# A two-group decoder step on one core: a per-tile head and two more FFN steps in a woven attention stretch

## The chip, the core and the metric

The kernel runs on one core of a Trainium2 chip. The metric is the device time of one execution in microseconds. The median of three runs of the kernel before is 2487.3 us (2486.04 to 2487.68). A core has a matmul engine (PE, with PEld for its weight loads), a vector engine (DVE), a scalar engine (ACT), a general engine (POOL) and a queue engine that issues transfers (SP). Each works through its own instructions in order; where one needs another's result it waits.

## What is computed

One inference step of a decoder trunk with two layers over two groups: a prompt of 1024 tokens and 8 samples of one token, with width 1024, all in float32. Layer 0 mixes by a gated recurrence, layer 1 by stick-breaking attention over keys and values that all tokens share; both add attention into 256 memory tokens and a SwiGLU FFN, with a norm before and after each sub-layer. Cut to what matters here:

```python
def rmsnorm(x, g):
    y = xf * lax.rsqrt(jnp.mean(xf * xf, axis=-1, keepdims=True) + EPS)
    return (y * g).astype(x.dtype)

def swiglu(h, w_gu, w_down):
    gate, up = jnp.split(h @ w_gu, 2, axis=-1)
    return (jax.nn.silu(gate) * up) @ w_down

for l in range(DEPTH):
    hn = rmsnorm(h, g[0])
    if l < N_A:
        mix, S = a_mixer(hn, w_in_a[l], ...)
    else:
        mix = b_mixer(hn, w_in_b[l - N_A], sb_bias[l - N_A], k_all, v_all, ...)
    h = h + rmsnorm(mix, g[1])
    h = h + rmsnorm(swiglu(rmsnorm(h, g[2]), w_gu[l], w_down[l]), g[3])
```

## The kernel before

The prompt is cut into two groups of 512 tokens; the 8 samples ride with group 1, whose tiles are 520 wide. Activations lie with the 1024 features in eight blocks `x0` to `x7` of 128 rows. Each float32 operand is split into a rounded high part (ACT, `L204`, `L225`, `L1024`) and the rest (DVE, `L205`, `L226`, `L1025`), and each product is three matmuls: high by high, high by low, low by high. A weight tile of 256 KB is loaded by SP, split by ACT and DVE, and used by PE.

**The head** (`start(0, ...)`, `L317` on). Four tiles of 128 tokens are loaded. `rms_rows` squares a tile and sums it (on ACT at `L310`, for every second tile on DVE at `L308`), takes the root by a logarithm and an exponential on ACT (`L311`, `L312`) and scales the tile on DVE (`L313`). Then, for each of the eight feature blocks, four transposes on PE (`L340`) fill one bank, and ACT and DVE scale and split it into `x` (`L343`, `L344`). The norm gains come from `par`, a transpose of the packed parameters (`L148`, `L149`). The first products are those for V (`rows_proj`, `L1017`): eight weight tiles, twelve matmuls each at `L1030`.

**Weaving.** A stage is a generator that yields after each step. `weave` always takes the next step of the stream whose number of steps taken over its weight is smallest; a stream that runs out drops away. This fixes the order in which work is handed over. The framework then places the instructions on each engine, which moves some of them past each other, and the engines keep that order.

**Layer 1, group 1 attention** (`L1570`). Three streams are woven: prompt attention (`sb_prompt`, 28 steps, and `mem_attn`, 8) with weight 40; sample attention (38 steps) with weight 39; and the FFN of group 0 with weight 30. A step of `sb_prompt` makes scores on PE (`L1324`), a bias and clip on DVE (`L1335` to `L1339`), an exponential and a logarithm on ACT (`L1310`, `L1311`), a scan and a subtraction on DVE (`L1344`, `L1346`), an exponential on ACT (`L1347`), four transposes on PE (`L1353`), a copy on ACT (`L1355`) and the value matmuls on PE (`L1358`). Sample steps put products and sums on DVE (`L924`, `L925`, `L936`, `L937`) and a small matmul on PE (`L938`).

The FFN (`class ffn`, `L688`) is cut into five parts of 5, 5, 4, 4 and 4 hidden blocks. A part makes one step for each hidden block (gate and up, 48 matmuls of 512 columns) and four steps for the down-projection (two output blocks each, 24 matmuls, added to the residual by DVE at `L391`). Parts 0 to 2 and the first 4 steps of part 3, its hidden blocks, run in this weave: 9 + 9 + 8 + 4 = 30 steps. The other 4 steps of part 3 are held back.

**After it.** `o1.mm` is the output projection of group 1. `o1.finish` (17 steps) takes its norm (the sum over partitions is a matmul at `L247`, root at `L248`, `L249`), adds the residual in eight steps (`L372`, `L378`, squares summed at `L258`), takes the next norm and scales and splits the eight blocks (`normed`: `L264`, `L225`, `L226`) that the last FFN reads. It is woven, 17 to 12, with the 4 steps of part 3 that were held back and the 8 of part 4. Then the last FFN begins (`ffn_w`, `L1578`): three hidden blocks by plain products (`gate_up_q`, `L455`; their up halves are multiplied in at `L468`), during which DVE also prepares sums of the normed blocks (`sums_w`, `L289`, `L297`), and from the fourth block on products by these sums (`gate_up_w`, `L502`). `f0.finish` and the stores of group 0 are woven into it.

```python
    weave(
        (chain(b1.sb(), b1.mem()), 40), (chain(b1.sb_sample(), b1.mem_sample()), 39),
        (chain(f0.part(0), f0.part(1), f0.part(2), islice(p3, 4)), 30),
    )
    o1 = out_proj(1, 1, A, True)
    weave((o1.mm(b1.xo), 8), (ws, 9))
    weave((o1.finish(), 17), (chain(p3, f0.part(4, True)), 12))
```

Of the kernel before, what the change touches and what calls it, by code (L numbers as in the profile page):

```python
# [23 lines left out]
def tile_decoder(  # L24
# [25 lines left out]
    def nm(s):  # L50
        uid[0] += 1
        return f"{s}_{uid[0]}"
# [45 lines left out]
    def NS():  # L98
        return nsp.tile([P, 512], F32, tag="ns", name=nm("ns"))
# [21 lines left out]
    def S():  # L121
        return smp.tile([P, 512], F32, tag="s", name=nm("s"))
# [21 lines left out]
    nc.vector.memset(epsb, EPS)  # L144
    xsraw = const.tile([P, ND, NB], F32, name="xsraw")
    par = const.tile([P, P], F32, name="par")
    pp = S()
    nc.tensor.transpose(pp[:, :P], prow, ident)  # L148
    nc.scalar.copy(par, pp[:, :P])  # L149

    def gcol(l, i, k):
        o = (l * 4 + i) * ND + k
# [151 lines left out]
    def rms_rows(xt, n, dve=False):  # L304
        ss = small([P, 1], tag="rr")
        junk = M().rearrange("p a n -> p (a n)")[:n, :D]
        if dve:
            nc.vector.tensor_tensor_reduce(junk, xt, xt, 1.0, 0.0, ALU.mult, ALU.add, ss[:n])  # L308
        else:
            nc.scalar.activation(junk, xt, AF.Square, accum_out=ss[:n])  # L310
        nc.scalar.activation(ss[:n], ss[:n], AF.Ln, scale=1.0 / D, bias=epsb[:n])  # L311
        nc.scalar.activation(ss[:n], ss[:n], AF.Exp, scale=-0.5)  # L312
        nc.vector.tensor_scalar(xt, xt, ss[:n], None, op0=ALU.mult)  # L313

    made, now = [None], [None]

    def start(g, out):  # L317
        if g:
            xtok.append(rpool.tile([P, CH, D], F32, tag="r", name="xtok1"))
            for tb in range(CH):  # L320
                nc.sync.dma_start(xtok[g][:, tb, :], x_prompt[0, g * G + tb * P : g * G + (tb + 1) * P, :])
            xs = C().rearrange("p a n -> p (a n)")[:NB]
            nc.sync.dma_start(xs, x_sample.rearrange("b o d -> (b o) d"))
        for tb in range(CH):
            rms_rows(xtok[g][:, tb, :], P, g == 0 and tb % 2 == 1)
            yield
        if g:
            ps = S()
            for k in range(ND):
                nc.tensor.transpose(ps[:, k * NB : (k + 1) * NB], xs[:, k * P : (k + 1) * P], ident[:NB, :NB])  # L330
            nc.vector.tensor_copy(xsraw, ps[:, : ND * NB].rearrange("p (k t) -> p k t", k=ND))
            rms_rows(xs, NB)
            pn = S()
            for k in range(ND):
                nc.tensor.transpose(pn[:, k * NB : (k + 1) * NB], xs[:, k * P : (k + 1) * P], ident[:NB, :NB])
            yield
        for k in range(ND):
            ps = S() if k % 2 else NS()
            for tb in range(CH):
                nc.tensor.transpose(ps[:, tb * P : (tb + 1) * P], xtok[g][:, tb, k * P : (k + 1) * P], ident)  # L340
            x = X(g)
            gk = gcol(0, 0, k)
            nc.scalar.activation(x[:, 0, :G], ps, AF.Copy, scale=gk)  # L343
            made[0] = nc.vector.scalar_tensor_tensor(  # L344
                x[:, 1, :G], ps, gk, x[:, 0, :G].bitcast(F32), op0=ALU.mult, op1=ALU.subtract
            )
            if g:
                pk = pn[:, k * NB : (k + 1) * NB]
                nc.scalar.activation(x[:, 0, G:], pk, AF.Copy, scale=gk)
                nc.vector.scalar_tensor_tensor(  # L350
                    x[:, 1, G:], pk, gk, x[:, 0, G:].bitcast(F32), op0=ALU.mult, op1=ALU.subtract
                )
            out.append(x)
            yield
# [662 lines left out]
    def rows_proj(W, m0, xt, dst):  # L1017

        pb = [mmp.tile([P, 2, 512], F32, tag="mm", name=nm("mm")) for _ in range(2)]
        for k in range(ND):  # L1020
            raw = wraw.tile([P, 512], F32, tag="w", name=nm("w"))
            nc.sync.dma_start(raw, W[k * P : (k + 1) * P, m0 : m0 + H * P])
            ws = wspl.tile([P, 2, 512], F32R, tag="ws", name=nm("ws"))
            nc.scalar.copy(ws[:, 0, :], raw)  # L1024
            nc.vector.tensor_sub(ws[:, 1, :], raw, ws[:, 0, :].bitcast(F32))  # L1025
            for i in range(2):
                for wi, (xi, s) in enumerate(((0, 0), (1, 0), (0, 1))):
                    for a in range(2):
                        c = 2 * i + a
                        nc.tensor.matmul(  # L1030
                            pb[i][:, a, :], xt[k][:, xi, c * P : (c + 1) * P], ws[:, s, :],
                            start=(k == 0 and wi == 0), stop=(k == ND - 1 and wi == 2),
                        )
            if k % 2:
                yield
        nc.scalar.copy(dst[0][:, :, :512], pb[0])
        nc.vector.tensor_copy(dst[1][:, :, :512], pb[1])
# [493 lines left out]
    def rest():  # L1531
# [36 lines left out]
    f0 = ffn(0, 1, o0.x)  # L1568
    p3 = f0.part(3)
    weave(  # L1570
        (chain(b1.sb(), b1.mem()), 40), (chain(b1.sb_sample(), b1.mem_sample()), 39),
        (chain(f0.part(0), f0.part(1), f0.part(2), islice(p3, 4)), 30),
    )
    o1 = out_proj(1, 1, A, True)
    weave((o1.mm(b1.xo), 8), (ws, 9))
# [37 lines left out]
```

## Time and profile before

| | us |
|---|---|
| median of three runs | 2487.3 |
| the profiled execution | 2488.67 |
| its span, first to last instruction | 2487.0 |
| V phase of the head ends | 39.39 |
| attention of layer 1, group 1, woven with the FFN | about 1597 to 1950 |
| `o1.mm` and `o1.finish` with the rest of the FFN | 1950 to 2110.05 |
| the last FFN begins | 2110.05 |

The profile is one execution. The page shows the busy time of each engine; the chain that ended last, followed back from the end; groups of instructions with their line. Views by stretch give, for a window, the busy time of PE, PEld, DVE, ACT and POOL with the number of instructions in brackets, then the granted PE clock (1.00 is full), the share of the transfer engines and their GB/s. Views in order of time give start, duration, engine, line, operation, written tile `<-` read tiles, sizes, and in brackets the idle time just before and who ended it. Matmuls overlap, so their single durations are longer than their pace; the pace is a stretch over its count.

### The profile page before, as it was taken

The page shows a single profiled execution, that of the slowest core. Times are in us where ns is not written, and L with a number is a line of the kernel's source. Part 1 is how long each engine was busy: PE and PEld are TensorE (multiplying, and loading weights), DVE is VectorE, ACT ScalarE, POOL GpSimd, SP SyncE. Part 2 cuts the span into 40 slices and gives each one's busy share as a digit, 9 for nine tenths or more (in the row PEclk, how much of TensorE's full clock was granted, in tenths as well). Part 3 has the DMA queues.
Part 4 walks back from the last instruction along what each step waited for, and adds up shares of the span by engine and source line. Part 5 has one row for each costly group of instructions (what it writes and reads, how often), then busy time and mean ns, then how long its engine had stood idle before and what let it go on. Part 6 is the DMA issues. An engine that isn't in the chain of part 4 may idle for free.

```text
span 2487.0 us, 42201 instructions
## 1 busy us (share of the span) xinstructions
PE 2456.4 (99%) x15971; PEld 2177.2 (88%) x15971; DVE 1615.4 (65%) x2942; ACT 1213.0 (49%) x2328; POOL 178.8 (7%) x316
## 2 busy tenths in 40 slices
PE   8999999999999999999999999999999999999998
PEld 6888888877879998899999989876777888999998
DVE  5867556754777685655755675777687466855666
ACT  5437544243435554555444554554554445654445
POOL 1000101100000000111200102111000100000000
PEclk9999999999999999999999999999999999999999
DMA  5354666546745437767666649745253473464552
GB/s 188 114 166 111 158 190 157 133 129 163 213 146 144 141 119 224 202 163 184 163 194 172 195 127 276 226 143 154 80 175 113 131 203 119 142 187 146 147 148 74
DMA packets 530503, 395.29 MB, mean 159 GB/s; under 512 B 21237, under 2 KB 468802, under 8 KB 530298
## 3 DMA queue, kind: packets, MB, share of 16 engines
q1 hardware_dynamic: 501114, 312.88, 42.2%
q0 software_dynamic: 29184, 79.70, 13.9%
q8 instruction: 126, 2.06, 0.3%
q14 instruction: 79, 0.65, 0.1%
HBM read 362.69 MB, written 101.11 MB: 186 GB/s over the span
## 4 chain that ended last, share of the span: by engine, by line
PE 89%; DVE 5%; DMA 2%; issue 2%; ACT 2%; POOL 0%; SPq 0%; DVEq 0%; POOLq 0%; ACTq 0%
PE mm L218 48%; PE q L502 13%; PE q L639 8%; PE s L1162 2%; PE mm L1030 2%; PE q L455 2%; PE s L897 1%; PE s L866 1%; PE s L1358 1%; PE mm L815 1%; PE mm L842 1%; PE s L1324 1%; PE q L671 1%; PE s L890 1%; PE ns L938 1%
## 5 line engine op out<-in xcount | busy, mean ns | idle before, releaser
L218 PE MATMUL mm<-x,ws 128*128 128x260 f32 (+1 forms) x6240 | 1120.7, 336 | 1.7 <-DVE r L648 1.7
L218 PEld LDWEIGHTS mm<-x,ws 128*128 128x128 f32 x6240 | 940.8, 188 | 134.6 <-issue 10.3
L204 ACT CAST ws<-w 128x512 fp32r<-128x512 f32 (+1 forms) x652 | 382.9, 588 | 549.6 <-PE mm L218 382.9
L205 DVE TENSOR_TENSOR ws<-w,ws 128x512 fp32r<-128x512 f32 (+1 forms) x652 | 419.8, 648 | 276.6 <-ACT ws L204 265.8
L218 PE MATMUL mm<-m,ws 128*128 128x512 f32 (+1 forms) x1344 | 281.1, 361 | 0.1
L218 PEld LDWEIGHTS mm<-m,ws 128*128 128x128 f32 x1344 | 217.8, 188 | 39.5 <-issue 4.5
L639 PE MATMUL q<-m,ws 128*128 128x260 f32 (+1 forms) x1824 | 222.1, 282 | 0.3 <-DVE r L648 0.3
L639 PEld LDWEIGHTS q<-m,ws 128*128 128x128 f32 x1824 | 219.0, 188 | 1.8 <-DVE t L525 0.5
L493 DVE TENSOR_TENSOR ws<-w,ws 128x512 fp32r<-128x512 f32 x181 | 124.1, 690 | 90.2 <-ACT ws L492 86.5
L492 ACT CAST ws<-w 128x512 fp32r<-128x512 f32 x181 | 111.9, 621 | 105.9 <-PE q L639 34.5
L502 PE MATMUL q<-x,ws 128*128 128x260 f32 (+1 forms) x1188 | 157.8, 282 | 0.0
L502 PEld LDWEIGHTS q<-x,ws 128*128 128x128 f32 x1188 | 148.6, 188 | 0.0
L502 PE MATMUL q<-y,ws 128*128 128x260 f32 x912 | 119.4, 283 | 0.5 <-DVE t L468 0.5
L502 PEld LDWEIGHTS q<-y,ws 128*128 128x128 f32 x912 | 113.5, 188 | 0.8 <-DVE t L468 0.8
L455 PE MATMUL q<-x,ws 128*128 128x260 f32 (+1 forms) x720 | 88.9, 283 | 0.0
L455 PEld LDWEIGHTS q<-x,ws 128*128 128x128 f32 x720 | 87.0, 188 | 1.1 <-issue 0.9
L502 PE MATMUL q<-a,ws 128*128 128x260 f32 (+1 forms) x672 | 87.1, 282 | 0.7 <-DVE t L468 0.7
L502 PEld LDWEIGHTS q<-a,ws 128*128 128x128 f32 x672 | 83.2, 188 | 0.9 <-DVE t L468 0.9
L648 DVE TENSOR_TENSOR r<-r,q 128x260 f32<-128x260 f32 (+1 forms) x128 | 48.4, 420 | 47.3 <-PE q L639 47.3
L235 DVE TENSOR_SCALAR t<-mm 128x512 f32<-128x512 f32 (+1 forms) x58 | 40.1, 691 | 57.2 <-PE mm L218 56.8
L707 DVE TENSOR_TENSOR t<-t,mm 128x512 f32<-128x512 f32 (+1 forms) x46 | 31.7, 688 | 54.9 <-PE mm L218 54.9
L557 POOL DMA_DIRECT2D wsum<-in_w_gu x64 | 58.7, 936 | 112.0 <-DMA wsum<-wsum 93.8
(350 smaller groups left out, 2974.0 us busy)
## 6 DMA issues: line engine op xcount, KB each, us to landing
w<-in_w_gu SPq DMA_DIRECT2D x297, 256.0 KB, 3.5
w<-in_w_down SPq DMA_DIRECT2D x160, 256.0 KB, 2.8
wsum<-in_w_gu POOLq DMA_DIRECT2D x72, 512.0 KB, 6.4
w<-wsum SPq DMA_DIRECT2D x104, 256.0 KB, 3.2
w<-in_w_in_a SPq DMA_DIRECT2D x80, 256.0 KB, 3.0
w<-in_w_o SPq DMA_DIRECT2D x64, 256.0 KB, 2.8
wsum<-in_w_gu POOLq DMA_DIRECT2D x24, 640.0 KB, 7.2
wsum<-wsum POOLq DMA_DIRECT2D x24, 512.0 KB, 5.5
```

The lines of the kernel that those rows point to most:

```text
L204: nc.scalar.copy(ws[:, 0, :n, :], raw[:, :n, :])
L205: nc.vector.tensor_sub(ws[:, 1, :n, :], raw[:, :n, :], ws[:, 0, :n, :].bitcast(F32))
L218: nc.tensor.matmul(ps[:, a, : PW[g]], wt, xt[k][:, xi, o : o + PW[g]], start=(k == 0 and wi == 0), stop=(k == nk - 1 and wi == 2),)
L455: ins = nc.tensor.matmul(pp[a][:, :h], wt, xt[k][:, xi, a * h : (a + 1) * h], start=(k == 0 and wi == 0), stop=(k == ND - 1 and wi == 2),)
L492: nc.scalar.copy(w[:, 0, :], src)
L493: nc.vector.tensor_sub(w[:, 1, :], src, w[:, 0, :].bitcast(F32))
L502: nc.tensor.matmul(ps[:, :h], w[:, wj, k * P : (k + 1) * P], x[:, xi, :], start=(first and k == 0 and wi == 0), stop=(k == 3 and wi == 2), ...
L557: nc.gpsimd.dma_start(d, a, accum_op=ALU.add)
L639: nc.tensor.matmul(pp[a][:, :h], wt, mids[k][:, xi, a * h : (a + 1) * h], start=(k == 0 and wi == 0), stop=(k == nf - 1 and wi == 2),)
L648: nc.vector.tensor_add(d, d, pp[a][:, :h])
L1030: nc.tensor.matmul(pb[i][:, a, :], xt[k][:, xi, c * P : (c + 1) * P], ws[:, s, :], start=(k == 0 and wi == 0), stop=(k == ND - 1 and wi == 2),
L1162: nc.tensor.matmul(plv[:, hh, c, :], K_[:, hh, cs], rhs, start=True, stop=True)
```

## The change

Three things in the head, and the weights of the weave with two more FFN steps.

1. The last of the four token tiles is normed by `rms_halves`: ACT squares columns 0 to 511 and DVE 512 to 1023, ACT adds the two sums in the logarithm's bias, DVE scales the first 512 columns in two operations and ACT the other 512.
2. `turn` transposes feature blocks 0 to 2 of a tile as soon as that tile is normed, into three banks opened ahead; blocks 3 to 7 are transposed as before. The parameters' transpose moves behind the third tile, into a bank of the matmul pool.
3. The first two weight tiles of V are loaded ahead of the last tile's norm and split behind its scaling; `rows_proj` takes them from `first_w`. (`rows_proj` is also used by the K/V projection, where only the code moves into the two helpers.)
4. In the weave the weights go from 40, 39, 30 to 45, 39, 34, and the FFN's share from 30 steps to 32: two of the four down-projection steps of part 3 are no longer held back. The weave of `o1.finish` keeps its weights 17 and 12 and has 10 FFN steps.

```diff
-    pp = S()
-    nc.tensor.transpose(pp[:, :P], prow, ident)
-    nc.scalar.copy(par, pp[:, :P])
...
+    def rms_halves(xt):
+        sa, sd = (small([P, 1], tag="rr") for _ in range(2))
+        junk = M().rearrange("p a n -> p (a n)")[:, :D]
+        h = D // 2
+        nc.scalar.activation(junk[:, :h], xt[:, :h], AF.Square, scale=D**-0.5, accum_out=sa)
+        nc.scalar.activation(sa, sa, AF.Identity, bias=epsb)
+        nc.vector.tensor_tensor_reduce(junk[:, h:], xt[:, h:], xt[:, h:], 1.0, 0.0, ALU.mult, ALU.add, sd)
+        nc.scalar.activation(sa, sd, AF.Ln, scale=1.0 / D, bias=sa)
+        nc.scalar.activation(sa, sa, AF.Exp, scale=-0.5)
+        last = nc.vector.tensor_scalar(xt[:, : 2 * P], xt[:, : 2 * P], sa, None, op0=ALU.mult)
+        nc.scalar.activation(xt[:, h:], xt[:, h:], AF.Copy, scale=sa)
+        nc.vector.tensor_scalar(xt[:, 2 * P : h], xt[:, 2 * P : h], sa, None, op0=ALU.mult)
+        return last
+
+    def rows_load(W, k, m0):
+        raw = wraw.tile([P, 512], F32, tag="w", name=nm("w"))
+        nc.sync.dma_start(raw, W[k * P : (k + 1) * P, m0 : m0 + H * P])
+        return raw
+
+    def rows_split(raw):
+        ws = wspl.tile([P, 2, 512], F32R, tag="ws", name=nm("ws"))
+        nc.scalar.copy(ws[:, 0, :], raw)
+        nc.vector.tensor_sub(ws[:, 1, :], raw, ws[:, 0, :].bitcast(F32))
+        return ws
...
+    def turn(tb, pre):
+        if not pre:
+            pre.extend((NS(), S(), S()))
+        for k, ps in enumerate(pre):
+            nc.tensor.transpose(ps[:, tb * P : (tb + 1) * P], xtok[0][:, tb, k * P : (k + 1) * P], ident)
...
-        for tb in range(CH):
+        pre = []
+        for tb in range(CH - (g == 0)):
             rms_rows(xtok[g][:, tb, :], P, g == 0 and tb % 2 == 1)
+            if g == 0:
+                turn(tb, pre)
+            yield
+        if g == 0:
+            pp = mmp.tile([P, 2, 512], F32, tag="mm", name="pp")
+            nc.tensor.transpose(pp[:, 0, :P], prow, ident)
+            nc.scalar.copy(par, pp[:, 0, :P])
+            raws = [rows_load(w_in_a[0], k, 8 * P) for k in range(2)]
+            scaled = rms_halves(xtok[g][:, CH - 1, :])
+            with tc.issue_after(scaled.ins):
+                first_w.extend(rows_split(raw) for raw in raws)
+            turn(CH - 1, pre)
             yield
...
-            ps = S() if k % 2 else NS()
-            for tb in range(CH):
-                nc.tensor.transpose(ps[:, tb * P : (tb + 1) * P], xtok[g][:, tb, k * P : (k + 1) * P], ident)
+            ps = pre[k] if k < len(pre) else S() if k % 2 else NS()
+            if k >= len(pre):
+                for tb in range(CH):
+                    nc.tensor.transpose(ps[:, tb * P : (tb + 1) * P], xtok[g][:, tb, k * P : (k + 1) * P], ident)
...
-            raw = wraw.tile([P, 512], F32, tag="w", name=nm("w"))
-            nc.sync.dma_start(raw, W[k * P : (k + 1) * P, m0 : m0 + H * P])
-            ws = wspl.tile([P, 2, 512], F32R, tag="ws", name=nm("ws"))
-            nc.scalar.copy(ws[:, 0, :], raw)
-            nc.vector.tensor_sub(ws[:, 1, :], raw, ws[:, 0, :].bitcast(F32))
+            ws = first_w.pop(0) if first_w else rows_split(rows_load(W, k, m0))
...
     weave(
-        (chain(b1.sb(), b1.mem()), 40), (chain(b1.sb_sample(), b1.mem_sample()), 39),
-        (chain(f0.part(0), f0.part(1), f0.part(2), islice(p3, 4)), 30),
+        (chain(b1.sb(), b1.mem()), 45), (chain(b1.sb_sample(), b1.mem_sample()), 39),
+        (chain(f0.part(0), f0.part(1), f0.part(2), islice(p3, 6)), 34),
     )
```

More of the change, by code (lines that the diff above doesn't have):

```diff
@@ L313, in rms_rows @@
         nc.vector.tensor_scalar(xt, xt, ss[:n], None, op0=ALU.mult)
-    made, now = [None], [None]
+    def rms_halves(xt):
[20 more added lines that the diff above has]
+        return ws
+    made, now, first_w = [None], [None], []
+    def turn(tb, pre):
[3 more added lines that the diff above has]
+            nc.tensor.transpose(ps[:, tb * P : (tb + 1) * P], xtok[0][:, tb, k * P : (k + 1) * P], ident)
     def start(g, out):
```

## The prediction, made before the changed kernel ran

> **What bounds the kernel now.** I read the page first, then who waited for whom on the matmul engine, then busy times by stretch, then the instructions in order of time where the change bears.
>
> ```profile
> span 2487.0 us, 42201 instructions
> PE 2456.4 (99%) x15971; PEld 2177.2 (88%) x15971; DVE 1615.4 (65%) x2942; ACT 1213.0 (49%) x2328; POOL 178.8 (7%) x316
> ```
>
> The matmul engine (PE) is busy for 2456.4 of 2487.0 us, so 30.6 us are idle, and no matmul is added or removed beyond their order. Only three things can move the end: PE's idle time, a stretch in which its clock is halved, and new idle time. The profiled execution took 2488.67 us, 1.37 above the median of 2487.3; I make the sum against it and state the result from the median.
>
> PE's waits from 1560 us on, by line and releaser (total, times, longest), and the stretch in which the sample and prompt attention of layer 1 are woven with the FFN of group 0 (PE busy first):
>
> ```profile
> PE s L1353 <- ACT b L1347: 2.4, 5, 1.1
> PE s L1358 <- ACT b L1355: 2.2, 1, 2.2
> PE q L502 <- DVE t L468: 0.5, 1, 0.5
> ```
>
> ```profile
> 1597.00:1950.00 353.00, 347.81 (x1589) 260.49 (x1587) 260.46 (x400) 174.04 (x338) 25.93 (x24) 1.00 0.43 130
> ```
>
> So that weave holds 353.00 - 347.81 = 5.2 us of waiting, nearly all of it PE waiting for the scalar engine (ACT) inside stick-breaking attention. That is what the new weights can win. After it the whole trace has only a 0.5 us wait left where the last FFN begins, so anything later can only get worse. The largest of the waits, around 1732 us:
>
> ```profile
> 1732.04 1.12 ACT L204 CAST ws<-w 128x512 fp32r<-128x512 f32 x2
> ...
> 1733.07 0.57 ACT L1355 COPY b<-s 128x512 f32<-128x512 f32 x1
> ...
> 1733.70 2.08 PE L1358 MATMUL s<-b,a 128*128 128x128 f32 x8 [2.16 <-ACT b L1355]
> ```
>
> ```profile
> 1732.00:1736.00 4.00, 2.30 (x11) 2.30 (x12) 3.64 (x6) 2.45 (x6) 0.00 (x0) 0.68 0.47 118
> 1736.00:1740.00 4.00, 4.00 (x16) 3.02 (x16) 2.06 (x7) 1.66 (x3) 0.00 (x0) 0.89 0.61 209
> ```
>
> Two weight casts stood ahead of the copy that PE needed. The granted clock (third number from the end) then fell to 0.68 and 0.89 of full speed: 4 x 0.32 + 4 x 0.11 = 1.72 us of clock lost. A wait of 2.16 us therefore cost nearly 3.9.
>
> **Part 1, the head.** Part of the chain that ended last, then the engines in order of time:
>
> ```profile
> 11.89 2.35 PE s L340 x11
> ...
> 15.09 1.66 PE mm L1030 x4
> ...
> 17.19 1.38 PE mm L1030 x6
> 18.57 0.44 PE ns L340 x4
> ...
> 21.76 17.63 PE mm L1030 x76
> ```
>
> ```profile
> 7.35 3.07 SPq L1022 DMA_DIRECT2D w<-in_w_in_a  x5
> ...
> 8.78 1.22 DVE L308 CUSTOM_DVE_ANT_0 m<-xtok 128x1024 f32<-128x1024 f32 x1 [0.48 <-DMA xtok<-in_x_prompt]
> 8.91 0.20 ACT L312 ACTIVATE rr<-rr 128x1 f32<-128x1 f32 x1
> ...
> 9.93 1.43 DVE L313 TENSOR_SCALAR xtok<-xtok,rr 128x1024 f32<-128x1024 f32 x2
> ...
> 11.99 0.69 ACT L343 ACTIVATE x<-ns,par 128x512 fp32r<-128x512 f32 x1 [0.26 <-PE ns L340]
> ...
> 13.15 1.13 ACT L1024 CAST ws<-w 128x512 fp32r<-128x512 f32 x2
> ...
> 14.74 2.01 PE L1030 MATMUL mm<-ws,x 128*128 128x512 f32 x4
> ```
>
> A transpose takes 2.35/11 = 0.21 us here and 0.44/4 = 0.11 later; a V matmul 1.66/4 = 0.41 and then 17.63/76 = 0.23. PE runs at half speed until about 16.6 us. The last token tile lands by 8.78. Before, both scalings end at 9.93 + 1.43 = 11.36. Split, the vector engine (DVE) needs 0.61 for its half square and scales tile 2 about 0.5 earlier; ACT is free at 9.11 and takes as long for its half, then four small operations of 0.2 or a little more and a 512-column scaling of 0.6, ending near 11.4 (estimates from these rows). The norm itself gains nothing. What moves is the order: transposes of the first three blocks run per tile, ACT then copies the parameters and makes x0 (0.69) and the first weights (0.56), so the first V matmul can start near 13.1, not 14.74. At half speed that is worth 0.8, less a gap of 1 us that opens on PE ahead of it (0.5 at half speed), plus tile 2's transposes half a microsecond sooner (0.25): -0.6 us. Two V loads pass the bias and page-table loads in SP's queue, ahead of the 7.35 us at which V's loads began. Token data stand ahead of them there:
>
> ```profile
> biasp<-in_sb_bias SPq DMA_DIRECT2D x1, 2.0 KB, 4.7
> ```
>
> A 2 KB load took 4.7 us to land, so a later load waits for the tokens and doesn't delay them. The users of the two small loads come after the norm, so I cost their delay at nothing; losing that cover would cost one such landing on DVE. The parameters' transpose now uses a bank of the matmul pool; it is read out before V's second bank is wanted, so that costs nothing either, or a copy's length if it weren't. The other bound of the head: the gap of 1 us may keep PE at half speed for one period longer, the price of the dip above, 1.72, less 0.6: +1.1. I take -0.1.
>
> [...]
>
> **Part 2, the weave.** Steps go to the stream with the least progress over weight. Attention has 36 steps, samples 38, the FFN 30 and now 32. Their ends move from 36/40 = 0.90, 38/39 and 30/30 to 0.80, 0.97 and 0.94 of the weave. FFN per attention step stays at 0.75; only the sample work, which crowds DVE, thins out. On SP the FFN's loads and the samples' cache loads change places accordingly, on POOL only the source of a marker changes; neither engine's order ends a PE wait in these rows, so I cost that at nothing. In the built order (that of the finished program's instructions on each engine) the bare place of the 2.16 us wait has gained four FFN matmuls, but the second unit of the second head now follows the first after 4.3 us of PE work, and other close pairs stay. Bounds: all of 5.2 + 1.72 = -6.9, or nothing; I take a third, -2.3, because the waits are spread and only one of the seven sites is plainly relieved.
>
> **Part 3, what the two steps leave behind.** Four down-projections (48 matmuls) leave the stretch that covers the out-projection's finish, whose weights 17 and 12 stay while the FFN there shrinks from 12 steps to 10. The FFN is used up at 10/12 of that weave and nearly three norm steps are left without cover. In the built order the last norms (L264, L226 x) gather behind the final down-projections: from the evacuation of the second of these to the third L468 pair, DVE's queue has the same instructions as before plus 3 L264, 3 L226 x, 2 L289, 1 L297 and 1 L226 y. What they cost, and how full DVE is there before (third busy column):
>
> ```profile
> 2094.96 0.76 DVE L264 SCALAR_TENSOR_TENSOR n<-a,par,st 128x520 f32<-128x520 f32 x1
> ...
> 2111.56 0.75 DVE L264 SCALAR_TENSOR_TENSOR n<-a,par,st 128x520 f32<-128x520 f32 x1
> 2112.23 0.68 DVE L258 TENSOR_TENSOR st<-st,n 128x512 f32<-128x512 f32 x1
> ...
> 2113.43 0.69 DVE L226 TENSOR_TENSOR x<-n,x 128x520 fp32r<-128x520 f32 x1
> 2114.05 0.68 DVE L205 TENSOR_TENSOR ws<-w,ws 128x512 fp32r<-128x512 f32 x1
> 2114.65 0.42 DVE L297 TENSOR_TENSOR b<-b,b 128x260 f32<-128x260 f32 x1
> 2114.99 0.42 DVE L289 TENSOR_TENSOR b<-x 128x260 f32<-128x260 f32 x1
> ...
> 2122.32 1.28 DVE L205 TENSOR_TENSOR ws<-w,ws 128x512 fp32r<-128x512 f32 x2
> ...
> 2147.43 0.74 DVE L468 TENSOR_TENSOR t<-t,q 128x260 f32<-128x260 f32 x2
> ```
>
> ```profile
> 2094.96:2110.05 15.09, 15.09 (x67) 12.26 (x66) 14.78 (x26) 8.75 (x15) 0.00 (x0) 1.00 0.25 71
> 2110.05:2123.52 13.47, 13.46 (x107) 12.77 (x105) 12.81 (x26) 11.12 (x18) 0.00 (x0) 1.00 0.14 39
> 2123.52:2147.43 23.91, 23.91 (x203) 23.91 (x201) 23.91 (x56) 11.21 (x26) 0.00 (x0) 1.00 0.33 94
> ```
>
> ```profile
> 2087.79 22.42 PE L218 MATMUL mm<-m,ws 128*128 128x512 f32 x96
> 2110.05 2.91 PE L455 MATMUL s<-x,ws 128*128 128x260 f32 x23
> ...
> 2116.93 28.88 PE L455 MATMUL q<-x,ws 128*128 128x260 f32 x240
> ...
> 2148.22 3.14 PE L502 MATMUL q<-y,ws 128*128 128x260 f32 x24 [0.55 <-DVE t L468]
> ```
>
> Start to start, L264 takes 0.67 us, L226 on x 0.62, a 260-column operation 0.34. The extra work is 3 x 0.67 + 3 x 0.62 + 4 x 0.34 = 5.2 us, on an engine that was busy for 51.5 of the 52.5 us between the two points. PE has the same 72 matmuls of L218 and 288 of L455 to do from there. What is late first: the second tile's weights (the L205 pair of 2122.32). Before, they ended at 2123.0; PE, after 96 matmuls of 0.12 us and a sum matmul from 2110.05 on, wanted them at about 2122.5, and shows no wait. In the new order the first L468 pair and one L226 of m also stand ahead of them (1.3 us), which makes 5.2 + 1.3 = 6.5 us. PE is behind in order: all later gate, up and down products stand behind that wait. The 0.55 us at L502 goes, since PE is late by then: +6.0. A wait so long is also followed by a half-speed period, as the 2.16 us one was: +1.7. Together +7.7. Bounds: 5.2 less DVE's 1.0 us of room and the 0.55, without a clock loss, +3.7; and 6.5 - 0.5 plus two such periods of 1.7, and 0.9 that DVE may spend waiting for the last six evacuations (PE paces them at 12 x 22.42/96 = 2.8 us each, DVE's work up to the last is about 15.9 of those 16.8), +10.3. I stay near the middle.
>
> Sum: 2488.67 - 0.1 - 2.3 + 7.7 = 2493.97; from the median, 2487.3 + 5.3 = 2492.6 us. The bound for a change, about what a measurement of this kernel can tell from none, is 0.2%, 5.0 us: 2482.3 to 2492.3.
>
> **Rivals.**
> *The clock stays down.* After a wait of 6 us PE restarts inside a period and stays at half speed for a second one, and the weave wins nothing: 7.7 + 1.7 - 0.1 = +9.3, 2496.6. For it: one 2.16 us wait sufficed for 1.72. Against: the dip of before lasted one period.
> *The two sides nearly cancel.* The wait at the second tile's weights is 6.0 but broken up by earlier short waits for the normed blocks x4 to x7, so the clock holds, and half the weave's 6.9 comes back: 6.0 - 3.4 - 0.1 = +2.5, 2489.8. For it: the new order puts up-projection matmuls between gate matmuls there, so PE meets lateness of the normed blocks in pieces.
> *Faster: the late norms are hidden after all.* The place is the stretch from 2094.96 to 2147.43; the price, the 7.7. It decides by whether DVE, at each L205, is done before PE asks: if the 5.2 us fit because the norms start sooner than I place them, only head and weave count, -2.4 to -7.5, 2479.8 to 2484.9. Against: DVE was full in all of 23.91 us, and PE waited for it already.
> *The weights do nothing.* Where samples were not what held attention up, the weave's 5.2 stays; that is the upper end of the forecast's own range, 2494.9.
>
> **How the numbers follow.** Forecast 0.50, two thirds of it above 2492.3 since its bounds reach further up; clock stays down 0.16; cancelling 0.26; hidden 0.08, of which 0.05 lies below 2482.3, where the weave wins most of its bound too. Slower by over 0.2%: 0.34 + 0.16 = 0.50. Within: 0.16 + 0.26 + 0.03 = 0.45. Faster: 0.05. Range: from 2485.5, which leaves out most of the hidden case, to 2497.5, 0.9 above the worse rival; the forecast alone, 2489.5 to 2495.5, about half way to its bounds.
>
> **What would show it.** Part 1: the first L1030 starts near 13 us and the V phase ends about 0.6 us before 39.39, or a microsecond after. Part 2: idle PE time in the weave between 2 and 5 us, no wait of 2 us at L1358. Part 3: a PE wait of 4 to 6 us at L455, released by L205 or ACT's L204 on the second tile's weights, DVE without idle time around it, and a granted clock below 0.9 just behind it. It is wrong if PE runs through L455 without a wait, or if the weave's idle time grows.

## The result, and the profile after

| | median, us | runs | ratio to before, 95% interval |
|---|---|---|---|
| before | 2487.30 | 22 | |
| after | 2491.41 | 22 | 1.0018 (1.0012 to 1.0024) |

The changed kernel is 4.1 us slower, inside the 0.2% that the prediction calls no change, and 1.2 us below the 2492.6 it gave. The profiled execution of after took 2496.24 us, the slowest of its 22, so stretches are compared below, not whole spans. Much of its excess lies in one place just ahead of the attention weave, where PE waits for a transfer and the granted clock is then halved from 1591.0 to 1594.5 us; of the other profiled runs only head_again shows that wait, 0.7 us long:

```profile
1591.46 2.07 PE L1364 MATMUL s<-a,a 128*128 128x128 f32 x4 [2.60 <-DMA a<-ksc]
```

The page's head, to be held against the one of before:

```profile
span 2494.5 us, 42215 instructions
...
PE 2460.7 (99%) x15971; PEld 2180.7 (87%) x15971; DVE 1615.3 (65%) x2943; ACT 1211.2 (49%) x2331; POOL 177.4 (7%) x316
```

PE's idle time is 2494.5 - 2460.7 = 33.8 us (30.6 before), and PE's busy time has grown by 4.3 us without one more matmul. Most of that is clock: behind the head and before the last few microseconds, after has four half-speed periods of 3.4 us and before two. In after, the old lines L218, L455, L468, L502, L205, L225 and L1426 are L215, L499, L512, L546, L202, L222 and L1466; L204, L248, L249, L372, L378, L313 and L1030 are L201, L245, L246, L416, L422, L310 and L1070, and the transposes of L340 are L345 (blocks 0 to 2) and L384.

**The weave.** Busy times by stretch, from the first long run of FFN matmuls in the attention weave to the first gate matmul of the last FFN: before, then after.

```profile
1588.95:2110.05 521.10, 515.91 (x2501) 404.31 (x2499) 358.52 (x558) 253.45 (x470) 39.97 (x52) 1.00 0.49 142
```

```profile
1594.04:2109.79 515.75, 513.57 (x2500) 403.84 (x2499) 352.86 (x548) 249.35 (x465) 40.06 (x52) 1.00 0.49 142
```

The same matmuls (a few records are missing in each trace) take 5.35 us less; 3.0 of that is idle time (521.10 - 515.91 = 5.19, now 2.18).

**Behind it.** PE's waits of after from 1990 us to the end, then PE's instructions and the rows of DVE and ACT (order of time) where the last FFN begins:

```profile
PE s L1466 <- DVE r L422: 2.3, 2, 2.0
PE s L499 <- ACT x L222: 2.2, 1, 2.2
PE q L499 <- ACT ws L201: 1.1, 1, 1.1
PE q L499 <- DVE ws L202: 0.3, 1, 0.3
```

```profile
2109.79 3.03 PE L499 MATMUL s<-x,ws 128*128 128x260 f32 x24
...
2117.99 0.51 PE L499 MATMUL s<-x,ws 128*128 128x260 f32 x2 [2.23 <-ACT x L222]
...
2126.55 0.75 PE L499 MATMUL q<-x,ws 128*128 128x260 f32 x4 [1.11 <-ACT ws L201]
2129.33 0.33 PE L1466 MATMUL s<-ident,r 128*128 128x128 f32 x1 [2.03 <-DVE r L422]
...
2130.53 23.71 PE L499 MATMUL q<-x,ws 128*128 128x260 f32 x184 [0.27 <-DVE ws L202]
...
2155.91 3.14 PE L546 MATMUL q<-y,ws 128*128 128x260 f32 x24
```

```profile
2113.50 1.28 ACT L245 ACT_TABLE_LOAD   x1
...
2114.79 0.69 ACT L245 ACTIVATE st<-ns,epsb 128x512 f32<-128x512 f32 x1
2115.50 1.28 ACT L246 ACT_TABLE_LOAD   x1
2116.79 0.63 ACT L246 ACTIVATE st<-st 128x512 f32<-128x512 f32 x1
2117.33 1.14 ACT L222 CAST x<-n 128x520 fp32r<-128x520 f32 x2
2117.45 0.75 DVE L416 SCALAR_TENSOR_TENSOR r<-r,par,st 128x512 f32<-128x512 f32 x1 [2.22 <-ACT st L246]
...
2128.58 1.30 DVE L422 TENSOR_TENSOR r<-r,ht 128x512 f32<-128x512 f32 x2
2129.78 1.30 DVE L202 TENSOR_TENSOR ws<-w,ws 128x512 fp32r<-128x512 f32 x2
```

In before, ACT cast the last normed block ahead of that root (L248, L249):

```profile
2112.35 0.63 ACT L225 CAST x<-n 128x520 fp32r<-128x520 f32 x1 [0.63 <-DVE n L264]
2113.00 1.28 ACT L248 ACT_TABLE_LOAD   x1
```

And, in after, the stretch behind the waits (granted clock third from the end):

```profile
2128.00:2132.00 4.00, 2.13 (x9) 1.75 (x10) 4.00 (x9) 0.41 (x1) 0.00 (x0) 0.79 0.04 11
2132.00:2136.00 4.00, 4.00 (x28) 4.00 (x28) 3.02 (x10) 1.34 (x3) 0.00 (x0) 0.78 0.88 250
```

From the first L499 to the first L546 on `y` it takes 2155.91 - 2109.79 = 46.12 us; before it took 2148.22 - 2110.05 = 38.17: +7.95. Waits of 5.9 us lie there, in three places, against 0.55 before. Casts of two normed blocks stand on ACT behind the root of the *next* stage, two table loads and two activations from 2113.50 to 2117.4 us; DVE waits for the same root. Then the second tile's weights are late, and PE's transposes for the store of group 0 wait for a residual. The clock falls behind it: 4 x (0.21 + 0.22) = 1.7 us. Waits and clock make 5.4 + 1.7 of the 7.95; the other 0.9 is longer PE busy time in many short groups and was not put at one place.

**The head.** The first V matmul starts at 12.94 us, not 14.74, and the first matmul behind the V phase at 39.13, not 39.23.

```profile
12.94 1.22 PE L1070 MATMUL mm<-ws,x 128*128 128x512 f32 x2 [0.49 <-ACT ws L334]
...
14.66 3.63 PE L1070 MATMUL mm<-ws,x 128*128 128x512 f32 x9
...
20.98 18.31 PE L1070 MATMUL mm<-ws,x 128*128 128x512 f32 x78
39.13 3.16 PE L215 MATMUL mm<-x,ws 128*128 128x512 f32 x13
```

The nine matmuls at 14.66 still take 0.40 each on the mean, the 78 later ones 0.23: half speed lasts to 17.5 us here, to 16.56 in before. What that does is only seen over many runs, below.

### The profile page after: what moved, and what is told of

It is laid out like the page before. It is cut to its first block, busy times and chain, and to the rows that moved or that the text cites. A ratio compares the mean times of both kernels' runs of the same rounds, so it can differ in the third digit from the quotient of the medians.

```text
span 2494.5 us, 42215 instructions
## 1 busy us (share of the span) xinstructions
PE 2460.7 (99%) x15971; PEld 2180.7 (87%) x15971; DVE 1615.3 (65%) x2943; ACT 1211.2 (49%) x2331; POOL 177.4 (7%) x316
## 3 DMA queue, kind: packets, MB, share of 16 engines
q0 software_dynamic: 29184, 79.70, 13.8%
## 4 chain that ended last, share of the span: by engine, by line
PE 91%; DVE 4%; DMA 2%; ACT 2%; issue 1%; SPq 0%; POOL 0%; DVEq 0%; ACTq 0%
PE mm L215 49%; PE q L546 13%; PE q L683 8%; PE q L499 3%; PE s L1202 2%; PE mm L1070 2%; PE s L941 1%; PE s L1364 1%; PE s L1398 1%; PE s L910 1%; PE mm L859 1%; PE mm L886 1%; PE q L715 1%; PE ns L982 1%; PE s L934 1%
## 5 line engine op out<-in xcount | busy, mean ns | idle before, releaser
L215 PE MATMUL mm<-x,ws 128*128 128x260 f32 (+1 forms) x6240 | 1121.4, 337 | 1.7 <-DVE r L692 1.7
L215 PEld LDWEIGHTS mm<-x,ws 128*128 128x128 f32 x6240 | 941.9, 189 | 136.1 <-issue 10.3
L201 ACT CAST ws<-w 128x512 fp32r<-128x512 f32 (+1 forms) x652 | 383.0, 588 | 561.5 <-PE mm L215 398.0
L202 DVE TENSOR_TENSOR ws<-w,ws 128x512 fp32r<-128x512 f32 (+1 forms) x652 | 421.2, 651 | 272.1 <-ACT ws L201 258.8
L215 PE MATMUL mm<-m,ws 128*128 128x512 f32 (+1 forms) x1344 | 281.5, 362 | 0.9 <-DVE r L435 0.9
L215 PEld LDWEIGHTS mm<-m,ws 128*128 128x128 f32 x1344 | 217.7, 188 | 41.9 <-issue 3.2
L546 PE MATMUL q<-x,ws 128*128 128x260 f32 (+1 forms) x1188 | 157.9, 282 | 0.0
L546 PEld LDWEIGHTS q<-x,ws 128*128 128x128 f32 x1188 | 148.6, 188 | 0.0
L546 PE MATMUL q<-y,ws 128*128 128x260 f32 x912 | 119.3, 283 | 0.0
L546 PEld LDWEIGHTS q<-y,ws 128*128 128x128 f32 x912 | 113.5, 189 | 0.2 <-DVE t L512 0.2
L499 PE MATMUL q<-x,ws 128*128 128x260 f32 (+1 forms) x720 | 91.8, 287 | 1.4 <-ACT ws L201 1.1
L499 PEld LDWEIGHTS q<-x,ws 128*128 128x128 f32 x720 | 88.9, 191 | 2.9 <-ACT ws L201 1.3
L546 PE MATMUL q<-a,ws 128*128 128x260 f32 (+1 forms) x672 | 87.2, 282 | 0.7 <-DVE t L512 0.7
L546 PEld LDWEIGHTS q<-a,ws 128*128 128x128 f32 x672 | 83.2, 188 | 0.9 <-DVE t L512 0.9
L223 DVE TENSOR_TENSOR m<-t,m 128x512 fp32r<-128x512 f32 (+1 forms) x88 | 61.0, 693 | 7.6 <-ACT m L222 6.9
```

Source lines behind the costliest of these rows:

```text
L201: nc.scalar.copy(ws[:, 0, :n, :], raw[:, :n, :])
L202: nc.vector.tensor_sub(ws[:, 1, :n, :], raw[:, :n, :], ws[:, 0, :n, :].bitcast(F32))
L215: nc.tensor.matmul(ps[:, a, : PW[g]], wt, xt[k][:, xi, o : o + PW[g]], start=(k == 0 and wi == 0), stop=(k == nk - 1 and wi == 2),)
L223: nc.vector.tensor_sub(dst[1], src, dst[0].bitcast(F32))
L499: ins = nc.tensor.matmul(pp[a][:, :h], wt, xt[k][:, xi, a * h : (a + 1) * h], start=(k == 0 and wi == 0), stop=(k == ND - 1 and wi == 2),)
L546: nc.tensor.matmul(ps[:, :h], w[:, wj, k * P : (k + 1) * P], x[:, xi, :], start=(first and k == 0 and wi == 0), stop=(k == 3 and wi == 2), ...
```

## The experiments

All ratios are to the kernel before, with their 95% intervals. "Weave" is the stretch shown above up to the last FFN's first matmul, "start of the FFN" the one from there to L502 (L546) on `y`, both in the profiled run. The kernel before ran again beside each series of experiments, with medians of 2488.12, 2487.48 and 2486.01 us in the three, and a ratio is to the runs of its own series; so compare ratios, not medians.

| kernel | median, us | ratio | weave | start of the FFN |
|---|---|---|---|---|
| before | 2487.30 | 1 | 521.10 | 38.17 |
| after | 2491.41 | 1.0018 (1.0012 to 1.0024) | 515.75 | 46.12 |
| head_only | 2488.73 | 1.0006 (0.9997 to 1.0015) | 522.51 | 38.17 |
| head_again | 2487.51 | 1.0010 (1.0001 to 1.0019) | 521.21 | 38.17 |
| weights_only | 2480.30 | 0.9972 (0.9963 to 0.9981) | 514.40 | 38.16 |
| steps_only | 2494.11 | 1.0035 (1.0021 to 1.0049) | 520.99 | 46.08 |
| weave_only | 2490.59 | 1.0012 (1.0003 to 1.0021) | 515.06 | 46.21 |
| head_and_weights | 2482.01 | 0.9984 (0.9975 to 0.9994) | 518.14 | 38.16 |
| finish_10 | 2482.45 | 0.9975 (0.9966 to 0.9984) | 514.99 | 37.99 |
| finish_9 | 2481.25 | 0.9979 (0.9968 to 0.9989) | 515.62 | 37.75 |
| old_head_finish_10 | 2480.04 | 0.9974 (0.9964 to 0.9984) | 515.16 | 38.00 |
| less_dve | 2487.10 | 0.9997 (0.9988 to 1.0006) | 514.95 | 42.51 |
| late_root | 2485.78 | 0.9998 (0.9989 to 1.0007) | 515.30 | 38.90 |
| samples_35 | 2482.40 | 0.9994 (0.9985 to 1.0004) | 517.96 | 38.16 |

### One part at a time

The change has three parts: head, weights of the attention weave, two steps moved. Each was made alone.

```diff
 head_only: the changed kernel with
+        (chain(b1.sb(), b1.mem()), 40), (chain(b1.sb_sample(), b1.mem_sample()), 39),
+        (chain(f0.part(0), f0.part(1), f0.part(2), islice(p3, 4)), 30),
 weights_only: the kernel before with 45, 39, 34 and islice(p3, 4)
 steps_only: the kernel before with 40, 39, 30 and islice(p3, 6)
 weave_only: the kernel before with 45, 39, 34 and islice(p3, 6)
```

> Only the head is changed; the attention weave keeps 40, 39, 30 and the four held-back steps. Theory (the prediction's first part): -0.1 us, between -0.6 and +1.1, so a ratio of 0.9998 to 1.0004; first V matmul near 12.9 us, V phase over at 39.3. Rival (the head is what won back part of the end's 7.95 us): -3 us or more, a ratio below 0.999.

> Only the weights of the attention weave are changed (45, 39, 34); four steps of part 3 run in it as before and four stay for the norm after it, so the first 30 FFN steps interleave as in the changed kernel. Theory A (the thinner sample work is what shortened the weave by 5 us): the weave still gains 3 to 5 us and the wait at L455 of the last FFN is absent: -3 to -5 us, ratio 0.998 to 0.999. Rival B (the two added FFN steps fill the end of the weave, where only samples run): no gain or a loss of up to 3 us, with new PE waits in the last tenth of the weave; ratio 1.000 to 1.001.

> Only the held-back steps are changed: six of part 3 in the weave instead of four, weights 40, 39, 30 as before. Theory A (weave gains by its weights alone): the end costs 6 to 8 us as in the changed kernel and the weave gains at most 1: +5 to +8 us, ratio 1.002 to 1.003, with PE waits at L455 of the last FFN released by the second tile's weights and by the normed blocks. Rival B (the steps win the weave): +2 to +3, ratio 1.001.

> Weights and held-back steps as in the changed kernel, the head as before. Theory: the changed kernel's +4.1 us less the head's -0.1 to -0.3, so +4.2 to +4.5 us, ratio 1.0017 to 1.0018. If weights and steps act independently, it is the sum of the two kernels in which each is changed alone; rival: they act together (the steps help only where the new weights leave room), and the sum is off by more than 2 us.

The weights alone win: -7.0 us by the ratio, more than theory A's 5. The steps alone lose +8.7, a little more than forecast; the added FFN steps win nothing in the weave (520.99 against 521.10), so rival B falls. The whole loss of the change is in the two steps: the start of the FFN is 46.1 to 46.2 with six steps and the old finish, and 38.2 with four, whatever the head and weights are. The sum of the two parts is -7.0 + 8.7 = +1.7 us, both together measure +3.0 (0.7 to 5.2): they act independently as far as this resolves. Waits of PE from 1590 us on in weights_only:

```profile
PE s L1353 <- ACT b L1347: 1.6, 5, 0.4
PE q L502 <- DVE t L468: 0.5, 1, 0.5
PE s L1358 <- issue: 0.2, 1, 0.2
```

```profile
1584.30:2098.70 514.40, 512.66 (x2502) 403.89 (x2500) 357.86 (x558) 252.79 (x470) 40.14 (x52) 1.00 0.49 143
```

The 2.2 us wait at L1358 is gone, the five waits at L1353 have shrunk from 2.4 to 1.6 us in all, and no half-speed period lies in the weave. Idle time falls by 5.19 - 1.74 = 3.45; PE's busy time by 515.91 - 512.66 = 3.25, of which the period at 1733 us explains about 1.9 (L1358's eight matmuls 2.08 us long and 1.16 here, L1324's four 1.68 and 1.03, and 0.3 in the L218 behind them). The other 1.3 is spread over many small groups and was not put at one place. The gain is not the same in every execution: in head_and_weights, with the same steps and weights in this weave, PE waits 2.0 us at L1364 for DVE, which had waited 3.47 us for a load of cached values, and a half-speed period follows at 1712.8 us; its weave takes 518.14.

### Why the last FFN waited

```diff
 finish_10: the changed kernel with
-    weave((o1.finish(), 17), (chain(p3, f0.part(4, True)), 12))
+    weave((o1.finish(), 17), (chain(p3, f0.part(4, True)), 10))
 finish_9: the same with 9; old_head_finish_10: weave_only with 10
 less_dve: the changed kernel, in the normed blocks of o1.finish
-            split_to((x[:, 0, :n], x[:, 1, :n]), t[:, :n])
+                nc.scalar.copy(x[:, 0, :n], t[:, :n])
+                nc.gpsimd.memset(x[:, 1, :n].bitcast(F32), 0.0)
 late_root: the changed kernel with
-    weave((chain(f0.finish(False), ...), 17), (chain(f1.part(0), f1.part(1)), 7))
+    p = chain(f1.part(0), f1.part(1)); drain(islice(p, 1))
+    weave((chain(f0.finish(False), ...), 17), (p, 6))
```

> The changed kernel with the weaving of the last out-projection's finish at 17 to 10 instead of 17 to 12, so that the ten FFN steps left there last as long as its 17 steps. Theory (the norms lost their cover because the weights were left): the second tile's weights stand ahead of the residual on DVE again, the waits at L499 and L1466 of the last FFN (5.9 us) and the half-speed period behind them go; the stretch from the first L499 to the first L546 on y falls from 46.1 to 38 to 39.5 us, the whole to about 2480 to 2483, ratio 0.997 to 0.9985. Rival (the norm work itself, with 48 fewer matmuls to cover it, no longer fits whatever its order): that stretch stays above 43 us and the time above 2487.

> As finish_10 with 17 to 9: the norm runs ahead of the FFN steps. Theory: the same stretch at 38 to 39.5 us, within 1 us of finish_10; new waits could come at L215 on the down-projections' weights, if the norm's DVE work now stands ahead of them, up to 1 us. Rival (order doesn't matter, cover does): above 43 us, as in finish_10.

> The changed kernel, but the low parts of the eight blocks that the last norm leaves are not computed on DVE (set to zero on POOL), so eight subtractions of 0.61 us, 4.9 us in all, leave DVE's queue in the stretch; the weaves are those of the changed kernel. Theory (DVE's queue is what the last FFN waits for): the waits at L499 and L1466 fall from 5.9 to 2 us or less and the half-speed period goes, the stretch from the first L499 to the first L546 on y falls from 46.1 to 38 to 41; ratio to before 0.997 to 0.9995. Rival (the wait is a chain of latencies: sum over partitions, root, norm, split, with no matmuls left beside it): it stays above 44 and the ratio above 1.001.

> The changed kernel, but the last FFN's first hidden block is handed over ahead of the finish of group 0's FFN, whose root (two table loads and two activations on ACT, 3.9 us) and first residual steps (on DVE) thereby stand behind the last normed blocks and the second tile's weights; the weaves are those of the changed kernel. Theory (the first 2.2 us wait is ACT's root ahead of the casts of two normed blocks, the later ones the residual ahead of the second tile's weights on DVE; the 48 missing matmuls of cover are no more than the occasion): the stretch from the first L499 to the first L546 on y falls from 46.1 to 38.5 to 41 us with waits of 2 us or less in it, ratio to before 0.997 to 0.9985. Rival (eight normed blocks, of which three come after the last down-projection, are late by themselves): it stays above 43, ratio 0.999 or above.

With 17 to 10 or 17 to 9 nothing is left of the wait (38.0 and 37.8 us), and the kernel beats the one before, as was expected of both. So the norm fits with 48 fewer matmuls beside it; it was handed over too late. PE at the start of the last FFN in finish_10:

```profile
2104.23 3.86 PE L499 MATMUL s<-x,ws 128*128 128x260 f32 x31
...
2110.83 17.87 PE L499 MATMUL q<-x,ws 128*128 128x260 f32 x148
```

less_dve, which leaves the low parts of those eight blocks uncomputed, lies between theory and rival: 46.12 falls to 42.51, the waits at these lines from 5.9 to 2.4, and the half-speed period, which the theory had going, stays. So 3.6 of the 7.95 us go with DVE's queue. What stays is the other piece, PE waiting for ACT's casts of the normed blocks, and a clock loss behind it, though DVE had room (third busy column):

```profile
2108.82 0.98 PE L503 MATMUL s<-x,ws 128*128 128x260 f32 x6 [1.18 <-ACT x L264]
...
2111.28 1.31 PE L503 MATMUL s<-x,ws 128*128 128x260 f32 x6 [1.25 <-ACT x L264]
```

```profile
2108.00:2112.00 4.00, 1.94 (x13) 1.74 (x14) 1.47 (x4) 3.97 (x7) 0.00 (x0) 0.97 0.00 0
2112.00:2116.00 4.00, 4.00 (x23) 4.00 (x23) 4.00 (x11) 3.44 (x8) 0.00 (x0) 0.61 0.00 0
```

ACT is full there (3.97 of 4.00) with the next stage's root. late_root moves that root, and the residual that needs it, behind the casts: 38.90 us, inside the theory's 38.5 to 41. All of the norm's work is still there, so a change of order alone takes the wait away. But 2.1 us of it come back: from L546 on `y` to the end it takes 340.83 us, where the other kernels take 338.6 to 339.3. Against before's 338.78, 0.55 of this is PE's idle time and 1.5 its busy time. One transpose of the store more stands there (29 against 28), and the store's steps break up the L546 runs; whether that is the cause was not tested. Its ratio, 0.9998, misses my 0.997 to 0.9985; that forecast didn't follow from its own stretch: 1.0018 less 7.2 us is 0.9989.

### The head, and which matmuls the weights move

```diff
 head_and_weights: the changed kernel with islice(p3, 4)
 samples_35: the kernel before with
-    (chain(b1.sb_sample(), b1.mem_sample()), 39)
+    (chain(b1.sb_sample(), b1.mem_sample()), 35)
```

> The changed kernel with four steps of part 3 in the weave instead of six, that is the new head and the new weights alone. Theory: the end as before (38.2 us), the weave's gain of 6 to 7 us kept, the head worth nothing that can be told (-0.1): -6 to -7 us, ratio 0.997 to 0.9978. Rival (the new head costs 1 us or more, as the middle of its own interval says): -5 us or less, ratio 0.998 or above.

> New weights and six steps in the attention weave, the finish at 17 to 10, the old head. Theory: as finish_10, whose head is the new one: between equal to it and 2.5 us faster, ratio 0.9965 to 0.9975; the stretch from the first L455 to the first L502 on y at 38 us. It also says whether six held-back steps with the finish re-weighted beat four (the kernel with the weights alone, 0.9972): theory, no, within 1.5 us of it.

> The kernel before with the sample stream's weight 35 instead of 39 and nothing else: the same thinning of the samples (39 x 40/45 is 34.7), FFN to attention stays at 30 to 40 instead of 34 to 45. Theory (thinner samples are what takes the waits out of the weave): -5 to -7 us as with the new weights, ratio 0.997 to 0.998, no 2.2 us wait at L1358. Rival (the places of the FFN matmuls between attention steps decide, by the slightly larger FFN share): less than half of that, ratio 0.999 or above, and the 2.2 us wait at L1358 is still there.

> The kernel with the new head alone, once more, for a narrower interval: the theory of the prediction says -0.1 us; the three pairs of kernels that differ by the head so far put it at +0.8 to +1.7 us. Pooled with the first series: a middle below +0.5 us bears the theory out, one above +1 us says that the head costs something.

samples_35 misses the theory. By the ratio, thinner samples alone win 1.5 us (-1.0 to 3.7). Its twelve times fall into two groups, seven from 2480.6 to 2482.4 and five from 2486.1 to 2491.0; why is not known, and the profiled run is one of the faster seven. In it the weave holds 517.96 - 513.17 = 4.79 us of idle time, 0.4 less than in before, where weights_only holds 3.45 less:

```profile
1585.87:2103.83 517.96, 513.17 (x2502) 403.27 (x2499) 358.71 (x558) 252.72 (x470) 38.88 (x52) 1.00 0.48 142
```

A wait at L1358 is there again, ahead of the same eight matmuls as in before (the 97th to 104th of that line):

```profile
1723.34 1.12 ACT L204 CAST ws<-w 128x512 fp32r<-128x512 f32 x2
...
1725.39 0.62 ACT L225 CAST m<-t 128x512 fp32r<-128x512 f32 x1 [0.93 <-DVE t L707]
1725.91 0.58 ACT L1355 COPY b<-s 128x512 f32<-128x512 f32 x1
1726.55 1.16 PE L1358 MATMUL s<-b,a 128*128 128x128 f32 x8 [1.74 <-ACT b L1355]
```

ACT's copy stands behind a cast (L225) for which ACT itself waited 0.93 us on DVE. Four FFN matmuls cover the place in samples_35 as in weights_only, where PE waits there for 0.2 us at most; so they are not enough, and the order on ACT and DVE counts too. No half-speed period follows this wait of 1.74 us; in before the one behind the wait there cost about 1.9 of the 3.1 us by which the two profiled weaves differ. In these profiles, then, thinner sample work is a small part of the idle time that the new weights save. That the rest comes from where single steps fall in the queues is what is left, not something tested, and why 45, 39, 34 places them well stays open.

The head: two series of the same kernel give 1.0006 and 1.0010, together 1.0008 (1.0002 to 1.0014, the single interval over the root of two), +2.0 us. The other pairs that differ by the head agree in sign: after and weave_only +0.0006, head_and_weights and weights_only +0.0012, finish_10 and old_head_finish_10 +0.0001. So the head costs something, where -0.1 us was expected; head_and_weights comes out as its rival had it (0.998 or above), and old_head_finish_10 as its theory had it, within 1.5 us of weights_only. Where the cost arises, the 14 profiled runs suggest (us; the first column is the moment at which the trace's record of the granted clock goes to full for the first time):

| old head | full speed from | V ends | | new head | full speed from | V ends |
|---|---|---|---|---|---|---|
| weights_only | 14.07 | 37.88 | | head_only | 11.06 | 37.32 |
| samples_35 | 14.35 | 38.12 | | head_and_weights | 16.37 | 38.80 |
| steps_only | 15.39 | 38.46 | | late_root | 16.88 | 39.03 |
| before | 16.56 | 39.23 | | after | 17.50 | 39.13 |
| old_head_finish_10 | 16.69 | 39.39 | | head_again | 18.00 | 39.44 |
| weave_only | 16.96 | 39.47 | | finish_10 | 18.03 | 39.64 |
| | | | | less_dve | 19.35 | 40.14 |
| | | | | finish_9 | 19.92 | 40.72 |
| mean | 15.67 | 38.76 | | mean | 17.14 | 39.28 |

At an equal moment of release the new head is 0.4 us ahead (39.03 at 16.88 against 39.47 at 16.96). But the release comes at 16.4 us or later in seven of eight runs, and on the mean the V phase ends 0.5 us later, a difference that is smaller than the spread within either column. PE's last gaps before the release, in before and in head_again:

```profile
10.74 0.47 PE L340 MATMUL ns<-ident,xtok 128*128 128x128 f32 x1 [1.91 <-DVE xtok L313]
```

```profile
10.38 0.47 PE L345 MATMUL ns<-ident,xtok 128*128 128x128 f32 x1 [0.82 <-DVE xtok L310]
...
13.07 1.22 PE L1070 MATMUL mm<-ws,x 128*128 128x512 f32 x2 [0.52 <-ACT ws L334]
...
14.80 3.79 PE L1070 MATMUL mm<-ws,x 128*128 128x512 f32 x9
```

The old head's last gap ends at 10.3 to 10.9 us in its six runs, and the release comes 3.8 to 6.1 us later; the new head has one more gap, of 0.5 us, that ends at 12.9 to 13.8 in the seven, and the release comes 3.1 to 6.2 us after that. The record of the clock begins at the release. All later changes stand at whole multiples of 3.413 us from it (last section), so one can count back from it in such periods; that they lie so ahead of it too is inferred. In after, finish_10, finish_9, head_again and less_dve the new gap is the only idle time of PE in the period that ends 3.413 us before the release: at the end of that period, with 0.5 us idle in it, the clock was not freed, and at the end of the next one, without any, it was. So, by this count, in these five runs the new gap put off the clock. In head_only the period that ended at 11.06, ahead of that gap, held 0.4 us of idle time and the clock was freed. The gap at 10.03 in after is as short as the one at 9.96 there (0.27 and 0.26 us), but the period around it held 0.8 us of idle time.

A second cost may follow from the first, 500 us later; see the last section.

## Why the prediction came out

**The sum.** +5.3 was forecast, 4.1 measured. The forecast stood 0.3 us above the line of 0.2% that the prediction drew and gave half of its chance to the side above; the result lies below the line. A little slower was right, but with terms that were off in opposite ways: head -0.1 against about +2.0 by times (+0.5 at the end of V in the profiles); weave -2.3 against -6.0 (the mean of four profiled weaves with the old weights among the kernels above but samples_35 is 521.45, that of nine with the new ones 515.49); end +7.7 against +7.95. Errors of +2.1, -3.7 and +0.25 largely cancel, so that the sum came within 1.2 us is in part luck.

**Part 1** took the middle of two bounds. The step "first V matmul near 13.1" was right (12.81 to 13.78 in eight runs). The step that failed is the choice of -0.1: the gap ahead of it, though only 0.5 us long in most runs, did keep PE at half speed for one period longer in five of the eight runs, by the count back from the release, which is what its bound of +1.1 stood for.

**Part 2** was right in mechanism and mis-sized: "I take a third ... only one of the seven sites is plainly relieved". 6.0 of its bound of 6.9 was won, because waits at L1353 shrank too and the one long wait took its half-speed period with it. Idle 2.18 us and no 2 us wait at L1358 are what it asked for. Of its reasons, the four FFN matmuls at the bare place stand there in weights_only, where the wait is gone, but in samples_35 too, where it is not; thinner sample work took out only 0.4 us of idle time there.

**Part 3** has the right size and the right occasion (steps_only, and finish_10 undoes it), and names too few places. It asked for 4 to 6 us at L455 on the second tile's weights with DVE never idle. Measured were 1.4 us there, 2.2 on ACT's cast of a normed block and 2.3 at the store's transposes; DVE itself stood still for 2.22 us at 2117.45. The step that failed is the list of what is late: it counted DVE's instructions and left out that ACT's root and group 0's residual had changed places with the last norms. less_dve sizes the error: 3.6 of the 7.95 go with DVE's queue, and late_root shows that the order alone undoes the wait. The 1.7 us of clock came as said, though a wait of that length did not always bring it: none followed the one of 2.23 us at 2117.99.

**The rivals.** "The two sides nearly cancel" was right that waits would come in pieces and that the weave would give more; wrong that the clock would hold. It gave 2489.8, 1.6 below the result, about as far off as the forecast on the other side. "Clock stays down", "hidden" and "the weights do nothing" are refuted by the 1.7 us, steps_only and weights_only.

## What to carry to other kernels

A stage's price is paid by the stage that loses its cover: when steps are moved out of a weave, set its weights again (17 to 10 for 17 to 12 turned +4 us into -6 here), and test parts alone, since a gain of 7.0 and a loss of 8.7 looked like one small change. When work is handed over later, look at what it changes places with on *every* engine's queue, table loads of the next stage among them, not only at the fullest engine. The fastest versions here are the new weights with the old steps, 0.9972, and six steps with the finish at 17 to 10 and the old head, 0.9974; their intervals don't tell them apart.

## What the hardware showed beyond that

**Half speed without a wait.** The record of the granted clock gives the half-speed periods of before and after a length of 3.412 to 3.414 us at a share of 0.50, and all begin a whole number of times 3.4133 us after the first release: in before, released at 16.56, at 559.3 and 1733.5 us (159 and 503 periods), in after, released at 17.50, at 532.9, 560.2, 1591.0 and 2130.3 us (151, 159, 461 and 619). In each of the fourteen profiled runs the last fall of the clock, behind PE's last matmul, stands 720 to 725 such periods after the release, to within 0.1 us. Five of the eight runs with the new head have one 151 periods after the release, near 532 us, where PE shows no wait; none of the six old ones has it. PE's busy column is full and the clock is not (head_again):

```profile
532.00:536.00 4.00, 4.00 (x18) 2.35 (x18) 3.33 (x4) 0.39 (x1) 0.00 (x0) 0.68 0.80 232
```

Matmuls with eight rows (L1110) or eight columns (L1113; L1150 and L1153 with the new head) stand there. In the five runs they begin 0.0 to 1.0 us after a period's edge, in the other nine 1.1 to 2.8 us after it. From the start of the first L1110 to the start of the last it takes 73.6 us in weights_only and finish_9 without such a period, 75.1 in before with one, 76.7 in after with two: about 1.5 us each. So a head that shifts the release shifts what far later work meets. Between 525 and 615 us the eight runs with the new head hold ten half-speed periods, the six with the old one five: 0.4 more a run, an estimated 0.6 us, which with the 0.5 us at V makes about half of the +2.0. That this shift causes part of the head's cost is inferred from 14 runs, not tested; the rest is not accounted for.

Nor does the length of a wait tell by itself whether such a period follows. One began at about the end of waits of 2.16 us (before, L1358) and 2.0 us (head_and_weights, L1364), and of two of 1.18 and 1.25 us in less_dve (L503); none at the end of waits of 2.23 us in after (L499 at 2117.99) and 1.74 us in samples_35 (L1358). Around the periods near 532 and 560 us in after, and the one at 559 in before, PE shows no wait from 500 to 570 us. What sets a period off is not shown here.

**Table loads.** Each of the root's two activations had its own table load of 1.28 us, in after at 2113.50 and 2115.50, in before at 2113.00 and 2115.53; in after the second is 1.28 of the 3.9 us for which the casts of the normed blocks stood behind the root.
